# Query and key rows of a hybrid attention block laid out per head in DRAM, with more slots and raw weight buffers

## The chip, the core and the metric

The kernel runs on one core of a Trainium2 chip. The metric is device microseconds of one execution. Engines are named as in the profile: PE is TensorE, DVE VectorE, ACT ScalarE, POOL GpSimd, SP SyncE (here only a DMA queue).

## What is computed

One decoder block over 1024 tokens of width 1024: a root-mean-square norm, one input projection, three attention mixers side by side, an output projection with residual, and a squared-ReLU MLP (width 4096) with residual.

```python
def reference(x, norm_mix, norm_mlp, w_in, ..., w_out, w_up, w_down):
    h = rms_norm(x, norm_mix[l])
    proj = h @ w_in[l]
    a_q, a_kv, a_g, b_qkv, c_qkv = jnp.split(proj, PROJ_SPLITS, axis=-1)
    o_a = nsa_mixer(a_q, a_kv, a_g, ...)        # 4 heads: compressed, selected and window keys
    o_b = dilated_mixer(b_qkv, ...)             # 6 heads in 3 groups of dilation 1, 4, 16
    o_c = stick_breaking_mixer(c_qkv)           # 6 heads, strictly causal
    x = x + jnp.concatenate([o_a, o_b, o_c], axis=-1) @ w_out[l]
    h = rms_norm(x, norm_mlp[l])
    x = x + jnp.square(jax.nn.relu(h @ w_up[l])) @ w_down[l]
```

All heads have 64 dimensions; everything is float32.

## The kernel before

**Precision.** Every matmul operand is split into two parts, hi and lo (a cast on ACT at L103 and a difference on POOL or DVE at L112), and a product is hi·hi + hi·lo + lo·hi. A score needs 64 rows for each part, so hi and lo share the 128 partitions: a key tile is [hi; lo], 64 rows each. `scores` (L633) multiplies it once by the query tile `qh` = [hi; hi] and once by `ql` = [lo; lo], and adds both in PSUM; a masked score has a third small matmul.

**Two streams of work.** A generator `filler` computes the projections, pair of heads by pair of heads, then the output projection and MLP of the first half of the tokens. Between its steps the attention units (`Sb`, `Dil`, `Nsa`; half 0 are tokens 0 to 511, half 1 the rest) are emitted: `spend` hands each unit's cost to the filler. A scheduler then fixes the order on each engine. After the last unit, the second half's output projection and MLP remain: the last 510 us are nearly pure matmul.

**Through DRAM.** The projections' queries, keys and values do not stay in SBUF. `spill_qk` (L540) writes a pair's hi tile and lo tile, 128 rows (two heads) by 512 tokens each, into `q_d` and `k_d`, shaped [pair, hi or lo, 128, 1024]; `spill_v` (L565, L572) writes `v_d`. These stores are issued on the SP queue, between the weight loads. `load_heads` (L605) fetches them for a unit on the POOL queue, into "slots" of 128x1024 from a pool of 11. A query load (L609, L624) reads 64 rows of DRAM twice by an outermost dimension of step 0; a key load (L615, L627) has an outermost dimension of two for hi and lo. A value load (L616, L629) has 128 plain rows. The second-half queries of the NSA heads go through `nq_d` in the same way (L443, L759). `take`, `free` and `live` count slots, and `prefetch` starts the loads of the next units when enough of the 11 are free; the wait for a slot to come free stands on the POOL queue.

**Weights.** `load_w` (L140 on) fetches a group of the input projection in parts of 128x512 into a raw buffer `wraw` (two of them, L168), on the SP queue (L169), and `put` splits a part into `whi` and `wlo` at steps of 4 us of the planner's clock. With two parts in flight, the load of part i+2 is written behind the `put` of part i. In the first 10 us of the planner's clock the order of these loads is fixed as written (`in_order`), among the first weights `w` (L332) and the input `xr` (L349). Later the output projection and MLP weights are loaded at L1045 into `raw`.

Of the kernel before, what the change touches and what calls it, by code (L numbers as in the profile page):

```python
# [16 lines left out]
S, D, HD, DFF = 1024, 1024, 64, 4096  # L17
NB = S // 128
# [41 lines left out]
def tile_trunk(ctx, tc, x, xT, w_in, w_out, w_up, w_down, cw1, cw2, small, t_nsa, t_dil, out):  # L60
# [25 lines left out]
    nq_d = dram.tile([2, 2, 2, 64, 512], F32, name="nq_d")  # L86
    q_r, k_r, v_r, nq_r = [t.bitcast(F32R) for t in (q_d, k_d, v_d, nq_d)]
# [31 lines left out]
    slots = actx.enter_context(tc.tile_pool(name="slots", bufs=11))  # L119
# [12 lines left out]
    def slot(name, dt=F32R):  # L132
        return slots.tile([128, S], dt, tag="slot", name=name)
# [7 lines left out]
    def load_w(key):  # L141
# [69 lines left out]
    DMA, SB0 = 4.0, 8.0  # L211
    FLIP, START, END = 1.3, 5.0, 2.5
    SLOTS = 11
# [215 lines left out]
    def nsa_q(W_q, half):  # L429
# [6 lines left out]
        def fin(p):  # L436
            tp = pair_T(v2, 128 * p)
            if half == 1:
# [3 lines left out]
                for part, t in enumerate((hi, lo)):  # L442
                    nc.sync.dma_start(nq_d[p, part].rearrange("h d t -> (h d) t"), t.bitcast(F32))  # L443
                return
            nsa['q', 0, p] = hi, lo = [slot(n).rearrange("p (h t) -> p h t", h=2) for n in ("nqh", "nql")]
            for i, r in ((0, A), (1, B)):
                put(hi[A, i], lo[A, i], tp[r], qg[r, 2 * p + i:2 * p + i + 1])
                nc.scalar.copy(hi[B, i], hi[A, i].bitcast(F32))
                nc.vector.tensor_copy(lo[B, i], lo[A, i].bitcast(F32))
# [87 lines left out]

    def spill_qk(pair, j, cs, hi, lo):
        for part, t in enumerate((hi, lo)):
            nc.sync.dma_start((q_d, k_d)[j][pair, part, :, cs], t.bitcast(F32))  # L540
# [52 lines left out]
    def rows_of(t, *dims):  # L593

        return bass.AP(tensor=t.tensor, offset=t.offset, ap=[list(d) for d in dims])

    def load_heads(pair, half, heads=(0, 1)):

        q0, nk = 512 * half, 512 * (half + 1)
        ks = slice(0, nk)  # L600
        n = len(heads)
        hs = slice(heads[0], heads[0] + n)
        halves = lambda t: t.rearrange("p (h s) -> p h s", h=2)
        part, twice = (128 * S, 2), (0, 2)
        if n == 1:  # L605
            r = 64 * heads[0]
            qq = halves(slot("qq"))
            for i in range(2):
                nc.gpsimd.dma_start(qq[:, i], rows_of(q_r[pair, i, r:r + 64, q0:q0 + 512], twice, (S, 64), (1, 512)))  # L609
# [3 lines left out]
            else:  # L613
                k, v = slot("k"), slot("v")
            nc.gpsimd.dma_start(k, rows_of(k_r[pair, 0, r:r + 64, ks], part, (S, 64), (1, nk)))  # L615
            nc.gpsimd.dma_start(v, v_r[pair, heads[0], :, ks])  # L616
            return [(qq[:, 0], qq[:, 1], k, v)]
        qh, ql = [halves(slot(nm)) for nm in ("qh", "ql")]
        k, v = [[t[:, 0], t[:, 1]] if half == 0 else [t, slot(nm)]
                for nm in "kv" for t in [halves(slot(nm)) if half == 0 else slot(nm)]]  # L620
# [840 lines left out]
```

## Time and profile before

| | |
|---|---|
| median of 3 runs | 1473.87 us (1472.23 to 1474.32) |
| profiled execution, its own time | 1478.49 us |
| its span | 1476.7 us |
| mean granted clock of TensorE | 0.953 of full speed |
| PE busy | 1347.3 us (91%), 7241 matmuls |
| DVE, POOL, ACT busy | 836.8, 684.3, 647.7 us |
| DMA on the SP queue (hardware) | 136.45 MB in 91808 packets |
| DMA on the POOL queue (software) | 33.85 MB in 86656 packets |
| all packets | 178572, of them 89376 under 512 B |

The profile is of one execution, 4.6 us longer than the median of the runs. It is read by stage here: an opening to 54 us, the projections with the first units to 481 us, the units of half 0 and the NSA heads to 777 us, the last units beside the first half's output projection and MLP to 966 us, and the second half's output projection and MLP. A row of a timeline has the start, the length, the engine and line, the instruction and its tiles, and in brackets the idle time before it with what ended that.

### The profile page before, as it was taken

What the parts mean: (1) busy time and instruction counts of PE and PEld (TensorE: products, weight loads), DVE (VectorE), ACT (ScalarE), POOL (GpSimd) and SP (SyncE); (2) the same over time, 40 slices, a digit from 0 to 9 for tenths busy, and PEclk for the clock granted to TensorE, in tenths of its full rate; (3) what the DMA queues carried; (4) which work ended last, traced back from release to release, by engine and by line L of the source; (5) the groups of instructions that cost most, each with busy time, mean ns of one, the idle gap of its engine ahead of it and who ended that gap; (6) DMA issues with size and microseconds to landing.
All of it is one profiled execution on the core that took longest, in us unless ns stands there. A gap on an engine that the chain in (4) does not pass through costs nothing.

```text
span 1476.7 us, 21132 instructions
## 1 busy us (share of the span) xinstructions
PE 1347.3 (91%) x7241; PEld 1156.5 (78%) x7241; DVE 836.8 (57%) x1973; ACT 647.7 (44%) x1453; POOL 684.3 (46%) x614
## 2 busy tenths in 40 slices
PE   8887978688797999999997696999999999999998
PEld 6876978688786887888886585788888888888887
DVE  7365664468566998888885353783453332332333
ACT  6234554357454666555564142553343222222221
POOL 2123224434673424454556252534755555556553
PEclk9999989899798999999999798999999999999999
DMA  5697566852734422244548545224434333333332
GB/s 180 166 187 192 143 148 152 152 134 61 136 95 144 137 62 61 73 119 115 122 113 146 94 110 110 75 62 136 123 111 145 89 100 94 92 100 92 95 100 86
DMA packets 178572, 171.65 MB, mean 116 GB/s; under 512 B 89376, under 2 KB 105248, under 8 KB 178464
## 3 DMA queue, kind: packets, MB, share of 16 engines
q1 hardware_dynamic: 91808, 136.45, 32.5%
q0 software_dynamic: 86656, 33.85, 13.0%
q8 instruction: 57, 0.93, 0.3%
q14 instruction: 51, 0.42, 0.1%
HBM read 142.67 MB, written 27.30 MB: 115 GB/s over the span
## 4 chain that ended last, share of the span: by engine, by line
PE 67%; DMA 13%; DVE 11%; issue 4%; ACT 4%; SPq 1%; POOL 1%; DVEq 0%; ACTq 0%; POOLq 0%
PE pd L1094 25%; PE pd L1160 23%; DMA wraw<-in_w_in_dram 6%; PE pd L250 6%; PE ptp L684 3%; DMA k<-k_d 2%; PE pd L258 2%; PE po L705 2%; PE po L700 2%; PE pscore L642 1%; PE pscore L639 1%; DMA xch<-stx 1%; DMA wraw<-in_cmp_w_dram 1%; ACT whi L103 1%; DVE b L864 1%
## 5 line engine op out<-in xcount | busy, mean ns | idle before, releaser
L112 POOL TENSOR_TENSOR wlo<-raw,whi 128x512 fp32r<-128x512 f32 x264 | 351.1, 1350 | 370.9 <-ACT whi L103 365.6
L1094 PE MATMUL pd<-whi,hid 128*128 128x512 f32 x1120 | 381.6, 401 | 4.1 <-DVE acc L1099 2.6
L1099 DVE SCALAR_TENSOR_TENSOR acc<-pd,rs,acc 128x512 f32<-128x512 f32 x256 | 191.0, 747 | 117.5 <-PE pd L1094 116.6
L1094 PEld LDWEIGHTS pd<-whi,hid 128*128 128x128 f32 x1120 | 212.2, 189 | 51.9 <-DVE acc L1099 4.3
L103 ACT CAST whi<-raw 128x512 fp32r<-128x512 f32 x264 | 150.6, 619 | 180.7 <-issue 87.8
L1094 PE MATMUL pd<-wlo,hid 128*128 128x512 f32 x560 | 221.7, 396 | 0.0
L1160 PE MATMUL pd<-h_hi,whi 128*128 128x512 f32 x512 | 203.2, 397 | 0.2 <-ACT h_hi L105 0.2
L1160 PE MATMUL pd<-h_lo,whi 128*128 128x512 f32 x512 | 203.0, 398 | 0.0
L1160 PE MATMUL pd<-h_hi,wlo 128*128 128x512 f32 x512 | 202.3, 395 | 0.0
L1164 DVE TENSOR_TENSOR sqr<-sqr 128x512 f32<-128x512 f32 x64 | 49.4, 772 | 263.0 <-ACT sqr L1163 262.7
L250 PE MATMUL pd<-whi,hT_hi 128*128 128x256 f32 (+1 forms) x512 | 155.4, 307 | 15.7 <-DVE vs L114 7.4
L250 PE MATMUL pd<-wlo,hT_hi 128*128 128x256 f32 (+1 forms) x512 | 153.1, 300 | 1.4 <-DVE wlo L112 1.4
L250 PE MATMUL pd<-whi,hT_lo 128*128 128x256 f32 (+1 forms) x512 | 151.7, 298 | 0.0
L1163 ACT ACTIVATE sqr<-pd 128x512 f32<-128x512 f32 x64 | 38.2, 597 | 211.6 <-PE pd L1160 211.6
L1094 PEld LDWEIGHTS pd<-wlo,hid 128*128 128x128 f32 x560 | 106.3, 190 | 20.2
L250 PEld LDWEIGHTS pd<-whi,hT_hi 128*128 128x128 f32 x512 | 104.1, 204 | 17.3 <-DVE vs L114 8.0
L1160 PEld LDWEIGHTS pd<-h_hi,wlo 128*128 128x128 f32 x512 | 97.0, 190 | 22.5
L1160 PEld LDWEIGHTS pd<-h_hi,whi 128*128 128x128 f32 x512 | 97.1, 190 | 22.1 <-ACT h_hi L105 0.7
L1160 PEld LDWEIGHTS pd<-h_lo,whi 128*128 128x128 f32 x512 | 96.4, 189 | 21.3
L112 DVE TENSOR_TENSOR pTlo<-ptp,pThi 128x512 fp32r<-128x512 f32 (+2 forms) x160 | 101.1, 638 | 19.5 <-ACT pThi L103 18.5
L250 PEld LDWEIGHTS pd<-wlo,hT_hi 128*128 128x128 f32 x512 | 105.2, 206 | 1.6 <-DVE wlo L112 1.6
L250 PEld LDWEIGHTS pd<-whi,hT_lo 128*128 128x128 f32 x512 | 104.5, 204 | 0.0
(279 smaller groups left out, 2585.7 us busy)
## 6 DMA issues: line engine op xcount, KB each, us to landing
raw<-in_w_down_dram SPq DMA_DIRECT2D x128, 256.0 KB, 2.9
raw<-in_w_up_dram SPq DMA_DIRECT2D x124, 256.0 KB, 2.9
wraw<-in_w_in_dram SPq DMA_DIRECT2D x66, 256.0 KB, 3.0
k<-k_d POOLq DMA_DIRECT2D x12, 512.0 KB, 19.8
v<-v_d POOLq DMA_DIRECT2D x12, 512.0 KB, 16.1
qh<-q_d POOLq DMA_DIRECT2D x20, 256.0 KB, 11.4
ql<-q_d POOLq DMA_DIRECT2D x20, 256.0 KB, 13.0
v_d<-vs SPq DMA_DIRECT2D x32, 128.0 KB, 3.0
```

The source lines that it names most:

```text
L103: nc.scalar.copy(dst, src)
L112: eng.tensor_tensor(dst_lo, src, dst_hi.bitcast(F32), op=OP.subtract)
L250: nc.tensor.matmul(ps[:, :n], tokens(a, d, tb), b, start=(d == 0 and j == 0), stop=(d == 7 and j == 2))
L258: nc.tensor.matmul(ps, a, b[half][:, d], start=(d == 0 and j == 0), stop=(d == 7 and j == 2))
L684: nc.tensor.transpose(tp[:, off:off + 128], a, ident)
L700: nc.tensor.matmul(po[:, o0:o0 + w], vst, hi[:, src:src + w], start=(e == 0), stop=False)
L705: nc.tensor.matmul(*rest, start=False, stop=last and s not in held)
L1094: nc.tensor.matmul(ps, a[:, cs], b, start=(k == 0), stop=(k == last))
L1099: nc.vector.scalar_tensor_tensor(acc[:, tb, os_], ps, r2[:, t:t + 1], acc[:, tb, os_], op0=OP.mult, op1=OP.add)
L1160: nc.tensor.matmul(ps, a[:, ds], b[:, d], start=(d == 0 and j == 0), stop=(d == 7 and j == 2))
L1163: nc.scalar.activation(h, ps, AF.Relu)
L1164: nc.vector.tensor_tensor(h, h, h, op=OP.mult)
```

## The change

1. The pool of slots has 12 in place of 11, and there are four raw weight buffers in place of two (`RAWS`): `load_w` issues up to four parts at once, and part i+4 stands behind the `put` of part i.
2. `q_d`, `k_d` and `nq_d` hold for each head 128 rows [hi; lo]. `spill_rows` writes a 128-row tile as two stores of 64 rows, one for each head. A group's `spill_qk` issues four stores in place of two: 24 groups give 48 more, and the NSA queries 4 more, 104 in place of 52, all on the SP queue.
3. The query tiles in SBUF are q1 = [hi; lo] and q2 = [lo; hi]; keys stay [hi; lo]. The two matmuls of a score give hi·hi + lo·lo and lo·hi + hi·lo: the same four products, and the same number of matmuls.
4. Loads have plain rows: q1 in one DMA of 128 rows (both heads together), q2 in two of 64 rows, keys and values of half 0 in one DMA for both heads, of half 1 in one for each head. The POOL queue issues 86 loads in place of 104. No load has a leading dimension of 2 or a step of 0.
5. The scratch memory of the software-issued DMA is set to 8192 bytes.

```diff
@@ (slots, raw buffers)
+SLOTS = 12
+RAWS = 4
-    nq_d = dram.tile([2, 2, 2, 64, 512], F32, name="nq_d")
+    nq_d = dram.tile([2, 2, 128, 512], F32, name="nq_d")
-    slots = actx.enter_context(tc.tile_pool(name="slots", bufs=11))
+    slots = actx.enter_context(tc.tile_pool(name="slots", bufs=SLOTS))
@@ load_w
-            raw = wpool.tile([128, 2 * WMAX], F32, tag="wraw", bufs=2, name="wraw")[:, :m]
+            raw = wpool.tile([128, 2 * WMAX], F32, tag="wraw", bufs=RAWS, name="wraw")[:, :m]
-        raws = [load(p) for p in parts[:2]]
+        raws = [load(p) for p in parts[:RAWS]]
-                if i + 2 < len(parts):
-                    raws.append(load(parts[i + 2]))
+                if i + RAWS < len(parts):
+                    raws.append(load(parts[i + RAWS]))
@@ spills
+    def spill_rows(dst, step, t):
+        for h, rows in ((0, A), (1, B)):
+            ap = bass.AP(tensor=dst.tensor, offset=dst.offset + h * step, ap=[list(e) for e in dst.ap])
+            nc.sync.dma_start(ap, t[rows].bitcast(F32))
     def spill_qk(pair, j, cs, hi, lo):
-        for part, t in enumerate((hi, lo)):
-            nc.sync.dma_start((q_d, k_d)[j][pair, part, :, cs], t.bitcast(F32))
+        for rows, t in ((A, hi), (B, lo)):
+            spill_rows((q_d, k_d)[j][pair, 0, rows, cs], 128 * S, t)
@@ load_heads
+    def fetch(t, src):
+        nc.gpsimd.dma_start(t.bitcast(F32), src)
+    def fetch_q(q1, q2, src):
+        fetch(q1, src)
+        fetch(q2[A], src[B])
+        fetch(q2[B], src[A])
-        for i, t in enumerate((qh, ql)):
-            for h in heads:
-                r = 64 * h
-                nc.gpsimd.dma_start(t[:, h], rows_of(q_r[pair, i, r:r + 64, q0:q0 + 512], twice, (S, 64), (1, 512)))
-        for h in heads:
-            r = 64 * h
-            nc.gpsimd.dma_start(k[h], rows_of(k_r[pair, 0, r:r + 64, ks], part, (S, 64), (1, nk)))
-        for h in heads:
-            nc.gpsimd.dma_start(v[h], v_r[pair, h, :, ks])
+        q = [halves(slot(nm)) for nm in ("q1", "q2")]
+        fetch_q(*q, by_head(q_d[pair], qs))
+        for nm, d in (("k", k_d), ("v", v_d)):
+            if half == 0:
+                t = halves(slot(nm))
+                fetch(t, by_head(d[pair], ks))
+            else:
+                t = [slot(nm) for _ in heads]
+                for h in heads:
+                    fetch(t[h], d[pair, h, :, ks])
@@ the program
-    nc = _bacc.Bacc("TRN2", target_bir_lowering=False, num_devices=1)
+    nc = _bacc.Bacc("TRN2", target_bir_lowering=False, num_devices=1, dynamic_dma_scratch_size=8192)
```

Two places show how the order on a queue moves. The first is the SP queue in the opening: `wraw` are parts of the input projection's weights (L169 before, L170 in the change), `w_243` and `w_253` are weights of the first group (L332), and `xr` is the input. Before:

```order
L169 DMA wraw<-in_w_in_dram 128x512 x2
L349 DMA xr<-in_xT_dram 128x1024
L332 DMA w_243<-in_w_in_dram 128x512
L349 DMA xr<-in_xT_dram 128x1024
L332 DMA w_253<-in_w_in_dram 128x512
L169 DMA wraw<-in_w_in_dram 128x512 x2
L349 DMA xr<-in_xT_dram 128x1024 x3
L169 DMA wraw<-in_w_in_dram 128x512 x2
```

In the change:

```order
L170 DMA wraw<-in_w_in_dram 128x512 x4
L349 DMA xr<-in_xT_dram 128x1024
L170 DMA wraw<-in_w_in_dram 128x512
L332 DMA w_243<-in_w_in_dram 128x512
L349 DMA xr<-in_xT_dram 128x1024
L332 DMA w_253<-in_w_in_dram 128x512
L170 DMA wraw<-in_w_in_dram 128x512
L349 DMA xr<-in_xT_dram 128x1024 x3
L170 DMA wraw<-in_w_in_dram 128x512 x2
```

Four raw loads now stand together, and a fifth, which needs the first raw buffer back, stands ahead of `w_243`, the next `xr` and `w_253`.

The second is the POOL queue in the late stage, at the loads for the second dilated unit (`Dil(1, 1)`: queries qh and ql, or q1 and q2, keys and values of a head pair, and `qq` of a single head), between the differences `wlo` and `hid` of the output projection and MLP. Before:

```order
L624 DMA qh<-q_d 128x1x512
L112 TENSOR_TENSOR wlo<-raw,whi 128x512
L624 DMA qh<-q_d 128x1x512
L112 TENSOR_TENSOR wlo<-raw,whi 128x512 x3
L112 TENSOR_TENSOR hid<-sqr,hid 128x512
L112 TENSOR_TENSOR wlo<-raw,whi 128x512 x2
L112 TENSOR_TENSOR hid<-sqr,hid 128x512
L624 DMA ql<-q_d 128x1x512 x2
L627 DMA k<-k_d 128x1x1024 x2
L629 DMA v<-v_d 128x1024
L112 TENSOR_TENSOR wlo<-raw,whi 128x512 x2
L629 DMA v<-v_d 128x1024
```

In the change:

```order
L113 TENSOR_TENSOR wlo<-raw,whi 128x512 x4
L113 TENSOR_TENSOR hid<-sqr,hid 128x512
L113 TENSOR_TENSOR wlo<-raw,whi 128x512 x2
L113 TENSOR_TENSOR hid<-sqr,hid 128x512
L600 DMA k<-k_d 128x1024 x2
L600 DMA v<-v_d 128x1024 x2
L113 TENSOR_TENSOR wlo<-raw,whi 128x512 x2
L600 DMA qq<-q_d 128x512
L600 DMA qq<-q_d 64x512 x2
L600 DMA k<-k_d 128x1024
L600 DMA v<-v_d 128x1024
```

The pair's query loads have moved ahead of this piece, its two key loads and two value loads stand together, and the single head's queries are one load of 128 rows and two of 64. On TensorE, 42 matmuls of L1094 (L1100 in the change) stand between the score that sets free the last stick-breaking pair's first key slot and the first score that reads that slot's new keys; before there were 24.

## Rows read from the trace of the kernel before

**Rows 1.** The page, busy time of TensorE (us, share, instructions) and DMA in 40 slices.
```profile
PE 1347.3 (91%) x7241; PEld 1156.5 (78%) x7241; DVE 836.8 (57%) x1973; ACT 647.7 (44%) x1453; POOL 684.3 (46%) x614
...
DMA  5697566852734422244548545224434333333332
```

**Rows 2.** Windows: start:end, length, busy us of each engine, granted clock, DMA share, GB/s.
```profile
54.00:481.00 427.00, 356.01 (x2416) 332.82 (x2417) 256.46 (x795) 207.55 (x540) 175.80 (x190) 0.89 0.61 144
...
777.00:966.00 189.00, 150.88 (x740) 127.02 (x739) 98.24 (x208) 70.05 (x146) 79.73 (x67) 0.88 0.52 103
966.00:1476.70 510.70, 506.61 (x2245) 412.09 (x2244) 196.90 (x279) 163.57 (x306) 279.44 (x218) 1.00 0.34 103
```

**Rows 3.** Chain of waits that ended last, 54 to 481 us; start, us, what.
```profile
by line: DMA wraw<-in_w_in_dram 21.8%; PE pd L250 21.7%; PE pd L258 5.6%; issue 4.1%; DMA k<-k_d 3.7%; DMA xch<-stx 3.3%; DMA wraw<-in_cmp_w_dram 3.0%; PE ptp L684 2.5%; ACT whi L103 2.5%; DMA v_d<-vs 2.5%; DVE wlo L112 1.9%; SPq L572 1.8%;
...
75.63 15.76 DMA k<-k_d
...
193.82 12.26 DMA wraw<-in_w_in_dram
```

**Rows 4.** The page, DMA issues: count, KB each, median us to landing.
```profile
wraw<-in_w_in_dram SPq DMA_DIRECT2D x66, 256.0 KB, 3.0
k<-k_d POOLq DMA_DIRECT2D x12, 512.0 KB, 19.8
```

**Rows 5.** DMA view, 190 to 207 us, issues and landing.
```profile
wraw<-in_w_in_dram SPq DMA_DIRECT2D x3, 256.0 KB, 9.5
...
k<-k_d POOLq DMA_DIRECT2D x2, 256.0 KB, 12.6
```

**Rows 6.** DMA view, 860 to 863.4 us, 40 slices and one load.
```profile
GB/s 0 0 0 0 0 0 0 0 0 0 337 145 0 48 96 193 193 241 193 482 193 482 193 241 482 289 434 386 386 434 338 243 101 103 32 33 80 53 52 52
...
v<-v_d POOLq DMA_DIRECT2D x1, 512.0 KB, 3.9
```

**Rows 7.** DMA view, 863.6 to 865.8 us, 40 slices.
```profile
GB/s 78 40 40 77 39 40 78 3 77 77 39 38 38 75 37 37 112 112 74 112 74 112 74 149 74 112 112 112 74 112 112 112 74 149 74 112 112 112 74 112
```

**Rows 8.** Timeline of TensorE about 820 us; start, us, instruction, idle before.
```profile
820.48 0.55 PE L639 MATMUL pscore<-k,qh 128*128 128x256 f32 x1 [16.92 <-issue]
...
823.44 0.55 PE L639 MATMUL pscore<-k,qh 128*128 128x256 f32 x1 [2.19 <-issue]
```

**Rows 9.** Timeline of TensorE about 899 us.
```profile
899.22 0.45 PE L639 MATMUL pscore<-k,qh 128*128 128x128 f32 x1 [13.30 <-DMA k<-k_d]
```

**Rows 10.** Timeline of the GpSimd queue, 794 to 829 us; start, us to issue.
```profile
796.38 1.59 POOL L627 DMA_DIRECT2D k<-k_d  x2
```

**Rows 11.** DMA view, 794 to 829 us, landing of the key loads.
```profile
k<-k_d POOLq DMA_DIRECT2D x3, 512.0 KB, 24.0
```

**Rows 12.** Windows, two stretches of the late stage at the lower clock.
```profile
808.24:828.72 20.48, 6.05 (x16) 4.75 (x17) 0.00 (x0) 0.00 (x0) 0.93 (x1) 0.50 1.00 126
...
890.16:903.81 13.65, 4.59 (x14) 3.95 (x15) 0.38 (x1) 0.33 (x1) 0.00 (x0) 0.50 0.61 123
```

**Rows 13.** Waits of TensorE, 54 to 481 us: total us, times, longest.
```profile
PE po L700 <- ACT pThi L103: 19.0, 4, 7.4
...
PE pscore L639 <- DMA k<-k_d: 5.5, 1, 5.5
```

**Rows 14.** Waits of the SyncE queue, whole span.
```profile
SPq L169 <- DVE wlo L112: 69.3, 25, 15.7
```

**Rows 15.** Timeline of the SyncE queue, 3 to 20 us.
```profile
6.38 0.70 SPq L332 DMA_DIRECT2D w<-in_w_in_dram  x1
...
16.24 0.94 SPq L169 DMA_DIRECT2D wraw<-in_w_in_dram  x2
```

**Rows 16.** Timeline of ScalarE, 12 to 26 us.
```profile
16.93 0.60 ACT L103 CAST whi<-w 128x512 fp32r<-128x512 f32 x1
```

**Rows 17.** Line 540, the spills: ns to issue, us to landing.
```profile
L540 SPq DMA_DIRECT2D k_d<-tlo x12: 319/358/667, 58.8 to 478.5; - x12
...
DMA to landing us min/median/max: 2.0/2.8/10.7
```

More of the change, by code (lines that the diff above doesn't have):

```diff
@@ L210, in tile_trunk @@
     pending = []
-    DMA, SB0 = 4.0, 8.0
+    DMA, SPILL = 4.0, 8.0
     FLIP, START, END = 1.3, 5.0, 2.5
-    SLOTS = 11
     live = [2]
@@ L441, in fin @@
                     put(hi[r], lo[r], tp[r], qg[r, 2 * p + i:2 * p + i + 1])
-                for part, t in enumerate((hi, lo)):
-                    nc.sync.dma_start(nq_d[p, part].rearrange("h d t -> (h d) t"), t.bitcast(F32))
+                for rows, t in ((A, hi), (B, lo)):
+                    spill_rows(nq_d[p, 0, rows], 128 * 512, t)
                 return
-            nsa['q', 0, p] = hi, lo = [slot(n).rearrange("p (h t) -> p h t", h=2) for n in ("nqh", "nql")]
+            nsa['q', 0, p] = q1, q2 = [slot(n).rearrange("p (h t) -> p h t", h=2) for n in ("nq1", "nq2")]
             for i, r in ((0, A), (1, B)):
-                put(hi[A, i], lo[A, i], tp[r], qg[r, 2 * p + i:2 * p + i + 1])
-                nc.scalar.copy(hi[B, i], hi[A, i].bitcast(F32))
-                nc.vector.tensor_copy(lo[B, i], lo[A, i].bitcast(F32))
+                put(q1[A, i], q1[B, i], tp[r], qg[r, 2 * p + i:2 * p + i + 1])
+                nc.scalar.copy(q2[B, i], q1[A, i].bitcast(F32))
+                nc.vector.tensor_copy(q2[A, i], q1[B, i].bitcast(F32))
         for p in range(2):
@@ L534, in tile_trunk @@
     t_sel, t_edge, t_cmp, vm = ntab[:, 0:S], ntab[:, S:S + 128], ntab[:, S + 128:S + 192], ntab[:, S + 192:S + 193]
+    def spill_rows(dst, step, t):
+        for h, rows in ((0, A), (1, B)):
+            ap = bass.AP(tensor=dst.tensor, offset=dst.offset + h * step, ap=[list(e) for e in dst.ap])
+            nc.sync.dma_start(ap, t[rows].bitcast(F32))
     def spill_qk(pair, j, cs, hi, lo):
[L539 to L540 removed]
+        for rows, t in ((A, hi), (B, lo)):
+            spill_rows((q_d, k_d)[j][pair, 0, rows, cs], 128 * S, t)
     def end_T(src, pair, j, half):
@@ L590, in spill_dqk @@
             later(6.0, lambda j=j, g=g: fin(j, g))
-    def rows_of(t, *dims):
-        return bass.AP(tensor=t.tensor, offset=t.offset, ap=[list(d) for d in dims])
+    def fetch(t, src):
[4 more added lines that the diff above has]
+        fetch(q2[B], src[A])
     def load_heads(pair, half, heads=(0, 1)):
[L599 to L602, printed above, removed]
+        qs, ks = slice(512 * half, 512 * half + 512), slice(0, 512 * half + 512)
         halves = lambda t: t.rearrange("p (h s) -> p h s", h=2)
-        part, twice = (128 * S, 2), (0, 2)
-        if n == 1:
-            r = 64 * heads[0]
+        by_head = lambda d, cs: d[:, :, cs].rearrange("h p s -> p h s")
+        if len(heads) == 1:
+            h = heads[0]
             qq = halves(slot("qq"))
-            for i in range(2):
-                nc.gpsimd.dma_start(qq[:, i], rows_of(q_r[pair, i, r:r + 64, q0:q0 + 512], twice, (S, 64), (1, 512)))
+            fetch_q(qq[:, 0], qq[:, 1], q_d[pair, h, :, qs])
             if half == 0:
@@ L614, in load_heads, with scores @@
                 k, v = slot("k"), slot("v")
[L615 to L616 removed]
+            fetch(k, k_d[pair, h, :, ks])
+            fetch(v, v_d[pair, h, :, ks])
             return [(qq[:, 0], qq[:, 1], k, v)]
[L618 to L632 removed]
+        q = [halves(slot(nm)) for nm in ("q1", "q2")]
+        fetch_q(*q, by_head(q_d[pair], qs))
+        kv = []
+        for nm, d in (("k", k_d), ("v", v_d)):
+            if half == 0:
+                t = halves(slot(nm))
+                fetch(t, by_head(d[pair], ks))
+                t = [t[:, 0], t[:, 1]]
+            else:
+                t = [slot(nm) for _ in heads]
+                for h in heads:
+                    fetch(t[h], d[pair, h, :, ks])
+            kv.append(t)
+        return [(q[0][:, h], q[1][:, h], kv[0][h], kv[1][h]) for h in heads]
+    def scores(q1, q2, n, k, masked=False):
         ps = ps_s()
@@ L755, in load @@
             if self.slots:
-                qs = nsa['q', 1, self.hp] = [slot(nm).rearrange("p (h t) -> p h t", h=2) for nm in ("nqh", "nql")]
-                for part, t in enumerate(qs):
-                    for i in range(2):
-                        nc.gpsimd.dma_start(t[:, i], rows_of(nq_r[self.hp, part, i], (0, 2), (512, 64), (1, 512)))
+                qs = nsa['q', 1, self.hp] = [slot(nm).rearrange("p (h t) -> p h t", h=2) for nm in ("nq1", "nq2")]
+                fetch_q(*qs, nq_d[self.hp].rearrange("h p t -> p h t"))
         def end(self):
@@ L769, in branch @@
             n, h = self.n, 2 * self.hp + i
-            (qh, ql), sl, st = [t[:, i] for t in nsa['q', self.half, self.hp]], SLOPES[6 + h], self.st[i]
+            (q1, q2), sl, st = [t[:, i] for t in nsa['q', self.half, self.hp]], SLOPES[6 + h], self.st[i]
             prev = None
@@ L849, in weights @@
         def weights(self, n, c0):
-            qh, ql, k, _ = self.head
+            q1, q2, k, _ = self.head
             Wn = 128 * (n + 1)
@@ L1220, in filler @@
         in_order(nc.sync.dma_start(dtab, t_dil))
-        later(SB0, lambda: done.add(('sb', 0)))
+        later(SPILL, lambda: done.add(('sb', 0)))
         W = next_w()
```

21 lines of the change are left out of this document (9 added, 12 removed).

## The prediction

> **What bounds the kernel now.** I read the page first: TensorE is busy for 1347.3 us of 1476.7 [rows 1], so some 129 us at most are idle time, and the high digits of DMA stand mostly in the first third. The windows by stage then say where the idle time lies [rows 2]: 427.0 - 356.0 = 71 us between 54 and 481 us, 189.0 - 150.9 = 38 us between 777 and 966 us, and only 4 us in the last 511 us. In the same two stages the granted clock is 0.89 and 0.88, in the last it is 1.00. A mean of 0.89 between the two levels shown, 1.0 (2.4 GHz) and 0.50 (1.2 GHz), is 22% of the 427 us, 94 us, at the lower level. So I ask what ends the waits of these two stages.
>
> In the middle stage the chain of waits [rows 3] names mostly loads: the raw weights 21.8% and 3.0%, keys 3.7%, the value spills 2.5%, together 31% of 427 us. The chain has 17 pieces of raw weights, which make 24.8% or 105.9 us. A raw weight load lands in 3.0 us as its median over the program [rows 4], but the pieces reach 12.26 us [rows 3]. What stands beside the long ones is the transfer of head loads: from 190 to 207 us three raw loads took 9.5 us, while key loads of the same size took 12.6 us [rows 5].
>
> Why are head loads slow? A 512 KB key load takes 19.8 us [rows 4]. A value load of the same size, on the same queue, with little beside it, took 3.9 us, and the 40 slices under it reach 482 GB/s [rows 6]. Two query loads alone, just behind it, moved 37 to 149 GB/s [rows 7]. The two forms differ in their outermost dimension: 128 rows for the value, a dimension of 2 for queries and keys. So **the form of the load, not its bytes, sets its time**, and it holds others up: in the middle stage the DMA engines are busy to 0.61 and move only 144 GB/s [rows 2].
>
> In the late stage TensorE stood still for 16.92 us, 2.19 us [rows 8] and 13.30 us [rows 9]. The first is put down to "issue", but the key loads were issued from 796.38 us on [rows 10], loads there land in 24.0 us [rows 11], and 796.4 + 24.0 = 820.4 is when the score began. The last is named as a key load. These 32.4 us wait for key loads, and behind them TensorE runs at 0.50 of its clock for 6.05 and 4.59 us of work [rows 12].
>
> **The change part by part.**
>
> *The loads' form (and per-head rows in DRAM).* All 80 query and key loads lose their outermost 2. Their price in the new form is not shown. From below it is the 3.9 us of the value load that stood nearly alone [rows 6], from above the 12.6 us that a 256 KB key load took in company [rows 5]. I take 4 to 6 us, near the value load, since that has the same rows and sizes; several will stand in one queue.
>
> Late stage: in the change 42 matmuls of 512 columns stand between the key slot's release and its next use, at the pace of the last stage (506.6 / 2245 = 0.226 us) [rows 2] 9.5 us; before it was 24, 5.4 us, against a landing of 24.0 us [rows 11]. A load of 4 to 6 us is covered, so the 32.4 us go; one of 12.6 us would leave about 3 us in each of two places. Of the work at half clock, half its time comes back: (6.05 + 4.59) / 2 = 5.3 us. I leave 2 us for what is late next, the value loads behind the keys on the GpSimd queue. Sum 32.4 + 5.3 - 2 = **-36 us**; bounds -24 (the stalls half filled again at the dearer price, and no clock) and -38.
>
> Middle stage: what the chain spends above the quiet landing is 105.9 - 17 x 3.0 = 54.9 us for raw weights. Keys are 3.7%, 15.8 us, one piece [rows 3], 11.8 us above a load of 4 us. Value spills are 2.5%, 10.7 us, 7.7 us above 3.0. Together 74 us. I take two thirds, **-50 us**. The rest goes to what ends next: ScalarE's casts and the transposes that wait for them, which already end 19.0 us of TensorE's waits, whereas a key load ends just 5.5 us of them by name [rows 13], and the small exchange through DRAM (`xch`, 3.3%). Bounds: 5.5 us, if all else is a chain of ScalarE and VectorE; and 71 us of idle time plus the price of the lower clock, at most 94 us x 0.83 busy / 2 = 39 us, so 110 us.
>
> *Four raw buffers.* SyncE waited 69.3 us for a difference to free a raw buffer, 25 times [rows 14]; with four parts in flight this wait moves behind the fourth. It is in the same chain as the raw landings, so I count it in the two thirds and add nothing. It has a price in the opening: a fifth raw load now stands ahead of `w_243`, and needs the first raw buffer, which came free at 16.24 us [rows 15]. So `w_243`, issued at 6.38 us before [rows 15], issues near 17.2 us, lands 3.0 us later [rows 4] at 20.2, and its cast, at 16.93 us before [rows 16], is 3.3 us late; the `xr` behind it too. I take **+4 us**. Bounds 0 (the cast of the first raw part comes earlier) and 10 (16.24 - 6.38, all of it on the path).
>
> *Doubled spills.* 52 more stores on SyncE. One takes 0.36 us to issue [rows 17], so 52 x 0.36 = 19 us of a queue that mostly waits. They stand ahead of weight loads, but with two more raw buffers a load of 3.0 us has slack. I take **+2 us**; bounds 0 and 19.
> The Trainium skill speaks against this part: "DMA: Bandwidth & Descriptors", Rules for kernel authors, calls two transfers to disjoint partition halves not worth it, since they share the same 16 engines and serialize, and asks for one transfer of 128 partitions. By that each pair costs a second transfer's time, not only its issue; the fourth case below is that. No run here shows a half store, so the trace neither agrees nor differs yet.
>
> *Twelfth slot, the queries' rows, fewer loads.* A slot more lets `prefetch` start a little earlier; q1 and q2 take the same matmuls; 18 loads fewer save about 0.8 us of issue each on GpSimd [rows 10], beside `wlo` work that is not late. In the middle stage they are part of the two thirds, in the late stage of the 36; nothing more.
>
> **The sum.** On the profiled execution: 1478.5 - 50 - 36 + 4 + 2 = 1398.5 us. That execution is 4.6 us above the median of the runs, so the median becomes **1394 us**.
>
> **The rivals.**
>
> *A, the forecast* (0.62): 1372 to 1420 us, from 28 us more or 20 us less given back in the middle stage and the shift of the small terms.
>
> *B, only the late stage gains* (0.16). For it: in the middle stage only 5.5 us of TensorE's waits end in a load by name [rows 13], and the casts and transposes would simply queue. Against it: 15.76 and 12.26 us pieces of the chain [rows 3] are plain transfers. Then -50 becomes 0: 1394 + 50 = 1444 us.
>
> *C, the middle stage loses all its transfer excess and most of its clock price* (0.13): 74 + 20 (half of 39) = 94 in place of 50, so 1394 - 44 = 1350 us. For it: the clock of 0.89 falls behind idle time. Against: casts and exchanges remain.
>
> *D, the half stores take the place of the load waits, slower* (0.05). The mechanism is one queue of stores whose halves run one after another: the 52 extra stores each cost a whole landing, at least 2.0 us [rows 17], and the weight loads behind them wait: 52 x 2.0 = 104 us against the 80 us won, 1394 + 104 = about 1498 us. It decides the sign when a pair costs more than 80 / 52 = 1.5 us beyond what it does now. Against it: a store takes 0.36 us to issue [rows 17], the queue goes on without its landing, and the same bytes move.
>
> *E, the change does not do what it says* (0.04). Loads of 64 rows, or with both heads in the middle dimension, might still move at the rate of the queries now [rows 7]. Then nothing is won and about 6 us are lost in the opening and the spills, while two raw buffers win a little: 1474 us.
>
> **How the numbers follow.** 0.2%, about 3 us, is what a measurement of this kernel can tell from no change. A, B and C lie below 1471 us: 0.62 + 0.16 + 0.13 = 0.91, and a hundredth of E: faster 0.92. E gives the rest of no change, 0.03. D is slower, 0.05. The range holds A, the nearer two thirds of B and of C, and the bounds of the small terms: 1346 to 1450 us. The forecast stays the likeliest, 1394 us.
>
> **What would show it.** In the changed profile, key and query loads of 512 KB should land in 4 to 8 us (19.8 before), packets under 512 B should fall by more than half, and the late stage should show no wait of TensorE over 5 us: its 38 us of idle time at most 8, its clock near 1.0. The middle stage should be about 377 us long with a DMA share well below 0.61 and raw loads on the chain near 3 us. The opening should end 3 to 5 us later, with a gap of ScalarE ahead of the cast of the third `w`. The sum is wrong if the middle stage keeps its 427 us although the loads are fast (then B), if SyncE's weight loads stand behind slow half stores (then D), or if key loads still take over 12 us (then E).

## The result and the profile after

The change takes 1377.71 us as the median of 4 runs (1374.45 to 1379.91), against 1473.05 us (1468.67 to 1474.32) of the kernel before on the same chip: a ratio of 0.9356, 95% interval 0.9328 to 0.9384. The medians differ by 95.3 us; the forecast was 1394 us, some 79 us faster.

The page of the profiled execution of the change: busy time, the granted clock in 40 slices, the packets, and the two large DMA queues.

```profile
span 1372.7 us, 21206 instructions
...
PE 1320.4 (96%) x7241; PEld 1128.5 (82%) x7241; DVE 852.1 (62%) x1973; ACT 648.5 (47%) x1453; POOL 660.2 (48%) x596
...
PEclk9999999899999999999999999999999999999999
...
DMA packets 102316, 171.37 MB, mean 125 GB/s; under 512 B 18240, under 2 KB 34112, under 8 KB 102208
...
q1 hardware_dynamic: 92640, 136.45, 34.2%
q0 software_dynamic: 9568, 33.56, 8.1%
```

TensorE is idle for 1372.7 - 1320.4 = 52 us, where it was 129 us [rows 1], and its busy time is 27 us shorter for the same 7241 matmuls, since the clock stays up. The packets of the software queue, which carries the head loads, fell from 86656 to 9568 for about the same bytes, and packets under 512 B from 89376 to 18240. By the packet records of the traces, 73344 of the software queue's packets before had 4 bytes, so hardly any data; in the change these are 1376. The page's DMA issues:

```profile
wraw<-in_w_in_dram SPq DMA_DIRECT2D x66, 256.0 KB, 3.3
k<-k_d POOLq DMA_DIRECT2D x17, 512.0 KB, 5.7
v<-v_d POOLq DMA_DIRECT2D x17, 512.0 KB, 5.0
q<-q_d POOLq DMA_DIRECT2D x10, 512.0 KB, 6.1
```

A 512 KB key load lands in 5.7 us, a query load in 6.1, a value load in 5.0; the key loads took 19.8 us [rows 4]. All loads of the heads together (shortest, median, longest):

```profile
DMA to landing us min/median/max: 3.2/6.0/10.2
```

To compare stages I cut both traces at the same counts of matmuls: the starts of the 233rd, 2649th, 4261st and 5001st, which in the kernel before are the bounds used above to within a us. Two windows of the kernel before at these bounds (columns as in [rows 2]):

```profile
54.60:481.10 426.50, 356.07 (x2416) 332.86 (x2417) 256.06 (x793) 207.19 (x540) 175.80 (x190) 0.89 0.61 144
777.50:966.70 189.20, 151.08 (x741) 127.18 (x740) 98.44 (x209) 70.65 (x147) 79.23 (x67) 0.88 0.52 103
```

The windows of the change:

```profile
0.00:58.40 58.40, 43.51 (x233) 35.91 (x233) 28.73 (x57) 29.40 (x46) 8.92 (x17) 0.95 0.50 158
58.40:408.70 350.30, 332.11 (x2416) 312.22 (x2417) 264.38 (x788) 206.35 (x542) 163.87 (x175) 0.97 0.63 175
408.70:712.40 303.70, 298.86 (x1612) 252.27 (x1611) 260.91 (x634) 176.05 (x410) 134.44 (x124) 0.99 0.32 96
712.40:864.10 151.70, 144.24 (x744) 120.31 (x742) 87.33 (x197) 67.78 (x139) 76.03 (x70) 0.99 0.44 130
864.10:1372.70 508.60, 501.69 (x2243) 407.75 (x2241) 210.78 (x300) 168.91 (x319) 276.96 (x213) 1.00 0.34 102
```

The middle stage went from 426.5 to 350.3 us, its clock from 0.89 to 0.97; the late stage from 189.2 to 151.7 us, its clock from 0.88 to 0.99. In the middle stage TensorE's idle time fell from 426.5 - 356.1 = 70.4 us to 350.3 - 332.1 = 18.2 us, and its busy time by 24.0 us for the same 2416 matmuls. The opening is 3.8 us longer, the stage between is 7 us longer, the last one 1 us shorter. The chain of waits from 54 to 410 us, about the middle stage, answers to [rows 3]:

```profile
by line: PE pd L250 24.0%; issue 4.7%; PE ptp L692 3.8%; PE pd L258 3.4%; DMA xch<-stx 2.7%; PE po L708 2.6%; DMA wraw<-in_w_in_dram 2.5%; DMA q_d<-thi 2.5%; PE po L713 2.4%; DMA k_d<-thi 2.1%; PE pscore L650 2.1%; DVE st L792 1.9%; ACT whi
...
205.38 9.01 DMA wraw<-in_w_in_dram
```

Parts of `w_in` are 2.5% of it, nearly all of that one piece of 9.01 us, and key loads are gone from the front; TensorE's own matmuls lead.

In the late stage no wait of TensorE for a load is left. Its longest waits there (total us, times, longest) are for an activation:

```profile
PE pd L1100 <- ACT sqr L1169: 3.6, 2, 3.0
```

The loads for the second dilated unit, on the GpSimd queue:

```profile
746.26 0.57 POOL L600 DMA_DIRECT2D k<-k_d  x1 [1.99 <-PE pscore L650]
748.76 0.55 POOL L600 DMA_DIRECT2D k<-k_d  x1 [1.93 <-PE pscore L650]
749.30 1.05 POOL L600 DMA_DIRECT2D v<-v_d  x2
```

and the landings there, which answer to the 24.0 us of [rows 11]:

```profile
k<-k_d POOLq DMA_DIRECT2D x3, 512.0 KB, 4.1
v<-v_d POOLq DMA_DIRECT2D x3, 512.0 KB, 6.0
```

The opening shows the fifth raw load ahead of the third first weight, on SyncE:

```profile
16.15 0.33 SPq L170 DMA_DIRECT2D wraw<-in_w_in_dram  x1
16.52 0.43 SPq L332 DMA_DIRECT2D w<-in_w_in_dram  x1
```

and what it does to the cast of that weight on ScalarE, which stood at 16.93 us [rows 16]:

```profile
19.43 0.62 ACT L104 CAST whi<-w 128x512 fp32r<-128x512 f32 x1 [2.23 <-DMA w<-in_w_in_dram]
22.64 1.34 ACT L106 ACTIVATE hT_hi<-xr,sm_t 128x512 fp32r<-128x512 f32 x2 [2.59 <-DMA xr<-in_xT_dram]
```

### The profile page after: what moved, and what is told of

Its sections match the earlier page's. It is cut to its first block, busy times and chain, and to the rows that moved or that the text cites. A ratio compares the mean times of both kernels' runs of the same rounds, so it can differ in the third digit from the quotient of the medians.

```text
span 1372.7 us, 21206 instructions
## 1 busy us (share of the span) xinstructions
PE 1320.4 (96%) x7241; PEld 1128.5 (82%) x7241; DVE 852.1 (62%) x1973; ACT 648.5 (47%) x1453; POOL 660.2 (48%) x596
## 3 DMA queue, kind: packets, MB, share of 16 engines
q0 software_dynamic: 9568, 33.56, 8.1%
## 4 chain that ended last, share of the span: by engine, by line
PE 72%; DVE 11%; DMA 5%; ACT 2%; issue 2%; SPq 1%; DVEq 0%; ACTq 0%
PE pd L1100 28%; PE pd L1166 24%; PE pd L250 6%; PE ptp L692 4%; PE po L713 2%; PE po L708 2%; DMA xch<-stx 2%; PE pscore L650 2%; PE pscore L647 2%; DVE b L870 1%; PE pd L258 1%; DVE pTlo L113 1%; DVE acc L1105 1%; DVE p L663 1%; DMA wraw<-in_w_in_dram 1%
## 5 line engine op out<-in xcount | busy, mean ns | idle before, releaser
L1100 PE MATMUL pd<-whi,hid 128*128 128x512 f32 x1120 | 381.2, 401 | 7.9 <-DVE acc L1105 3.8
L1100 PEld LDWEIGHTS pd<-whi,hid 128*128 128x128 f32 x1120 | 211.0, 189 | 56.8 <-DVE acc L1105 5.9
L1100 PE MATMUL pd<-wlo,hid 128*128 128x512 f32 x560 | 221.0, 395 | 0.0
L1170 DVE TENSOR_TENSOR sqr<-sqr 128x512 f32<-128x512 f32 x64 | 54.1, 845 | 226.4 <-ACT sqr L1169 226.4
L250 PE MATMUL pd<-whi,hT_hi 128*128 128x256 f32 (+1 forms) x512 | 148.1, 291 | 8.6 <-DVE vs L115 5.5
L250 PE MATMUL pd<-wlo,hT_hi 128*128 128x256 f32 (+1 forms) x512 | 146.4, 287 | 1.7 <-DVE wlo L113 1.7
L250 PE MATMUL pd<-whi,hT_lo 128*128 128x256 f32 (+1 forms) x512 | 146.2, 286 | 0.0
L1100 PEld LDWEIGHTS pd<-wlo,hid 128*128 128x128 f32 x560 | 105.6, 189 | 20.2
L104 ACT CAST pThi<-ptp 128x512 fp32r<-128x512 f32 (+2 forms) x160 | 86.9, 551 | 64.9 <-PE ptp L692 62.4
L250 PEld LDWEIGHTS pd<-whi,hT_hi 128*128 128x128 f32 x512 | 97.1, 190 | 9.6 <-DVE vs L115 5.9
L250 PEld LDWEIGHTS pd<-wlo,hT_hi 128*128 128x128 f32 x512 | 97.5, 191 | 2.6 <-DVE wlo L113 2.3
```

What stands on the lines that cost most here:

```text
L104: nc.scalar.copy(dst, src)
L250: nc.tensor.matmul(ps[:, :n], tokens(a, d, tb), b, start=(d == 0 and j == 0), stop=(d == 7 and j == 2))
L1100: nc.tensor.matmul(ps, a[:, cs], b, start=(k == 0), stop=(k == last))
L1170: nc.vector.tensor_tensor(h, h, h, op=OP.mult)
```

## The experiments

Two theories were set against each other. One: the outermost dimension of the loads sets their time, and by it the others'. The other: two more raw buffers and a slot more hid the long landings. Then come the price of half stores, of the fifth raw load, and whether more depth still pays. Each ratio is to runs of the kernel before that were measured beside that kernel (their medians lie between 1472.44 and 1475.91 us), while differences between two kernels of the table are differences of medians that were measured apart. All stage lengths are of the profiled execution, in us, between the same counts of matmuls; for raws_only that execution is 8.4 us faster than the median. The order of the work moves with each edit, so a few us between neighbouring stages mean little.

| kernel | median us | ratio to before, interval | opening | middle | next | late |
|---|---|---|---|---|---|---|
| before | 1473.05 | | 54.6 | 426.5 | 296.4 | 189.2 |
| the change | 1377.71 | 0.9356 (0.9328 to 0.9384) | 58.4 | 350.3 | 303.7 | 151.7 |
| layout_only | 1394.36 | 0.946 (0.941 to 0.9511) | 53.7 | 374.9 | 295.6 | 156.7 |
| raws2 (layout and slot) | 1388.59 | 0.942 (0.9381 to 0.946) | 54.0 | 368.3 | 304.1 | 150.9 |
| slots11 (layout and raw buffers) | 1384.75 | 0.9396 (0.9359 to 0.9434) | 58.0 | 356.2 | 299.3 | 159.3 |
| raws_only | 1444.76 | 0.9794 (0.9749 to 0.9839) | 57.3 | 387.8 | 298.2 | 180.6 |
| buffers_only (raw buffers and slot) | 1438.65 | 0.9761 (0.9713 to 0.9809) | 56.7 | 393.6 | 303.1 | 172.0 |
| keys2 | 1411.59 | 0.9575 (0.9528 to 0.9622) | 57.5 | 368.0 | 303.9 | 172.9 |
| store1 | 1537.3 | 1.0437 (1.0393 to 1.048) | 59.5 | 514.7 | 303.3 | 153.6 |
| halves | 1461.05 | 0.992 (0.9894 to 0.9947) | 52.9 | 413.8 | 298.0 | 184.5 |
| opening | 1378.54 | 0.9355 (0.9321 to 0.9388) | 60.8 | 350.6 | 305.3 | 152.0 |
| opening2 | 1371.18 | 0.9299 (0.9262 to 0.9336) | 51.1 | 352.5 | 306.8 | 152.6 |
| slots13 | 1373.93 | 0.9322 (0.9294 to 0.935) | 56.6 | 348.6 | 306.7 | 151.9 |
| raws6 | 1362.25 | 0.9242 (0.9216 to 0.9268) | 56.7 | 338.4 | 302.2 | 149.8 |

### The layout and the loads alone

```diff
-SLOTS = 12
-RAWS = 4
+SLOTS = 11
+RAWS = 2
```

> The change with two raw weight buffers and eleven slots, so the rows of queries and keys and the form of their loads alone. Theory (the form of the loads is what gained): 1380 to 1400 us, key loads landing in 4 to 8 us, no wait of TensorE over 5 us after 770 us. Rival (two more raw buffers and the slot are what hid the long landings): 1430 to 1450 us, with only the late stage's 36 us won.

Measured 1394.36 us, 81.5 us below the kernel before that ran beside it (1475.91 us) and within the theory's range. The late stage fell by 32.5 us and the middle stage by 51.6 us. The window of its middle stage shows 374.9 - 344.0 = 30.9 us of idle time:

```profile
53.70:428.60 374.90, 344.02 (x2416) 322.41 (x2417) 256.61 (x797) 204.32 (x538) 158.56 (x171) 0.94 0.59 163
```

The waits of ScalarE for raw weights did not all go with the long landings (total us, times, longest; first the kernel before, then this one):

```profile
ACT whi L103 <- DMA wraw<-in_w_in_dram: 83.9, 31, 8.9
...
ACT whi L104 <- DMA wraw<-in_w_in_dram: 50.3, 25, 5.9
```

On the chain of waits a raw part still has pieces like this one, where its load lands in 2.9 us in the median:

```profile
212.67 7.91 DMA wraw<-in_w_in_dram
```

So the new rows and the loads' form carry most of the gain, and with two raw buffers ScalarE still waits for a raw part 25 times, 2.0 us each: a part is only asked for when a buffer comes free.

### Buffers and slot alone, and the raw buffers alone

```diff
-slots = actx.enter_context(tc.tile_pool(name="slots", bufs=11))
+slots = actx.enter_context(tc.tile_pool(name="slots", bufs=12))
-    SLOTS = 11
+    SLOTS = 12
-raw = wpool.tile([128, 2 * WMAX], F32, tag="wraw", bufs=2, name="wraw")
+raw = wpool.tile([128, 2 * WMAX], F32, tag="wraw", bufs=4, name="wraw")
-raws = [load(p) for p in parts[:2]]
+raws = [load(p) for p in parts[:4]]
```

The diff is cut: the kernel before gets the smaller scratch memory too, and a second place that takes a raw buffer its number of buffers.

> The kernel before with four raw weight buffers, twelve slots and the smaller scratch memory; rows and loads as before. Theory (form of the loads): 1455 to 1478 us, the late waits of 13 to 17 us for key loads still there, TensorE idle for over 50 us between 54 and 481 us. Rival (depth of buffering): 1410 to 1440 us, with the idle time of the middle stage halved.

Measured 1438.65 us, 37 us faster: the theory's range was missed, and the rival's met in time, though the middle stage's idle time fell only from 70.4 to 47 us. The second kernel leaves the slots at eleven.

> The kernel before with four raw weight buffers and the smaller scratch memory, eleven slots, rows and loads as before. Theory (of the 37 us that buffers and slot won together, the raw buffers won the middle stage's 25 and the slot the late stage's 12): 1446 to 1455 us, the two late waits for keys still at 28 to 33 us, the casts' waits for raw weights under 15 us. Rival (raw buffers won it all): 1435 to 1442 us with the late waits at 20 us.

Measured 1444.76 us, 30 us faster than the kernel before that ran beside it (1474.95 us): the raw buffers won most of it. With them ScalarE's waits for raw weights are nearly gone although head loads are as slow as before:

```profile
ACT whi L103 <- DMA wraw<-in_w_in_dram: 9.9, 6, 3.0
```

But TensorE's wait for keys in the late stage stays with eleven slots,

```profile
785.01 0.55 PE L639 MATMUL pscore<-k,qh 128*128 128x256 f32 x1 [15.53 <-issue]
```

and with the twelfth slot it is shorter (the first of the two waits in buffers_only):

```profile
807.78 0.55 PE L639 MATMUL pscore<-k,qh 128*128 128x256 f32 x1 [9.89 <-issue]
```

The late stage shows the slot: 180.6 us with eleven, 172.0 with twelve. Neither theory was whole: depth hides long landings for 30 to 37 us, the loads' form removes them for 81 us, and the two overlap (37 + 81.5 is 118, together they win 95).

### The change without its raw buffers, and without its slot

```diff
-RAWS = 4
+RAWS = 2
```

> The change with two raw weight buffers in place of four. Theory: 1374 to 1390 us, since a raw load of about 3 us needs no deeper queue and the opening gets its 3.8 us back. Rival: 1400 us or more, with the waits of ScalarE's casts for raw weights back at tens of us.

```diff
-SLOTS = 12
+SLOTS = 11
```

> The change with eleven slots in place of twelve. Theory: 1374 to 1384 us, no difference that can be told, as no wait of TensorE for a load is left. Rival (the slot lets loads start early enough): 1390 us or more, with waits of TensorE for keys in the late stage.

Measured 1388.59 and 1384.75 us: on fast loads the two raw buffers still win 11 us and the slot 7 us, by the medians. The intervals of both ratios overlap with that of the change, by little for raws2, so neither size is firm. The raw buffers' 11 us is at the upper end of the theory's range for raws2, but the rival's sign came: the casts' waits for raw weights are back.

```profile
ACT whi L104 <- DMA wraw<-in_w_in_dram: 56.0, 30, 6.8
```

In the change this wait is 5.2 us, once. The slot's 7 us lies between the two guesses. The rival's sign, waits of TensorE for keys in the late stage, did not come; what the slot saves there is not settled. In the middle stage, from layout_only to slots11, the raw buffers take 374.9 to 356.2 us, and cost the opening 4.3 us.

### Keys alone with the old form

A key's hi and lo blocks stand 65 rows apart, so that a load keeps an outermost dimension of two. The keys of half 0, one load for two heads in the change, become one load for each head, five loads more; their stores stay half stores. The diff is cut to the new rows and the load.

```diff
+    k_d = dram.tile([6, 2, 2, 65, S], F32, name="k_d2")
+    def fetch_k(t, pair, h, ks):
+        b = k_d[pair, h, 0, 0:64, ks]
+        nk = ks.stop - ks.start
+        fetch(t, bass.AP(tensor=b.tensor, offset=b.offset, ap=[[65 * S, 2], [S, 64], [1, nk]]))
```

> The change with key loads alone back in the form with an outermost dimension of two: a key's hi rows and lo rows stand 65 rows apart in DRAM, so that the two blocks stay two; stores, queries, values, buffers and slots as in the change. Theory (the outermost two sets the load's time): key loads land in 10 to 20 us, TensorE waits for keys in the late stage again for 10 to 30 us, 1395 to 1430 us. Rival (it is the rows being stored by head, or the fewer loads, that gained): key loads land in 5 to 7 us, 1374 to 1384 us.

Measured 1411.59 us, 34 us slower than the change, with the late stage at 172.9 us in place of 151.7. The page's issues (KB each, median us to landing):

```profile
v<-v_d POOLq DMA_DIRECT2D x17, 512.0 KB, 11.7
k<-k_d POOLq DMA_DIRECT2D x12, 512.0 KB, 18.0
```

And in the timeline of TensorE in the late stage, the wait for the last stick-breaking keys, 13.30 us before the change [rows 9]:

```profile
857.68 0.44 PE L663 MATMUL pscore<-k,q 128*128 128x128 f32 x1 [8.39 <-DMA k<-k_d]
```

Key loads of the same bytes, from rows that lie alike but for the gap, land in 18.0 us in place of 5.7, and the value loads, whose form did not change, in 11.7 in place of 5.0. The DMA view from 760 to 800 us shows a raw weight caught in it:

```profile
v<-v_d POOLq DMA_DIRECT2D x3, 512.0 KB, 19.8
...
raw<-in_w_down_dram SPq DMA_DIRECT2D x3, 256.0 KB, 10.8
```

The theory holds: the outermost two sets the time of the load, and transfers beside it pay as well. The packet records of the two traces show how. On the GpSimd queue both kernels move the same 8192 packets of 4096 bytes, but in keys2 some are in flight during 260 us, for 50% of it at most four at a time; in the change during 156 us, for 15% of it at most four and for 57% twelve or more. So the data goes in the same pieces, with fewer of them at a time. Of the layout's 81.5 us, keys2 gives 34 back; queries alone in the old form were not tried, and that the rest is theirs is argued, not shown.

### One store with an outermost two, and half stores alone

```diff
-        for h, rows in ((0, A), (1, B)):
-            ap = bass.AP(tensor=dst.tensor, offset=dst.offset + h * step, ap=[list(e) for e in dst.ap])
-            nc.sync.dma_start(ap, t[rows].bitcast(F32))
+        ap = bass.AP(tensor=dst.tensor, offset=dst.offset, ap=[[step, 2]] + [list(e) for e in dst.ap])
+        nc.sync.dma_start(ap, t.bitcast(F32))
```

> The change with each pair of half stores of 64 rows written as one store of 128 rows, whose DRAM side has an outermost dimension of two. Theory (the outermost two slows a store as it slows a load, and 52 issues saved are worth little): stores land in 6 to 12 us in place of 2 to 3, and units that wait for them start later, 1380 to 1400 us. Rival (two half transfers serialize, one is better): 1365 to 1374 us.

Measured 1537.3 us, 160 us slower than the change, far beyond what either expected; all of it is in the middle stage, 514.7 us with a clock of 0.82. The mechanism expected was late stores; what the SyncE queue shows is a queue that stands (start, length of the issues):

```profile
170.95 15.15 SPq L170 DMA_DIRECT2D wraw<-in_w_in_dram  x5
...
188.05 7.17 SPq L570 DMA_DIRECT2D v_d<-vs  x1
```

and in the group of the stores' line, shortest, median and longest issue in ns:

```profile
L541 SPq DMA_DIRECT2D k_d<-tlo x12: 491/4730/7164, 65.5 to 574.8; - x12
```

Five raw weight loads behind such stores take 15.15 us to be issued, 3 us each, and the stores themselves are held for up to 7 us. In the change four raw loads behind half stores take 3.79 us, about 1 us each:

```profile
177.31 3.79 SPq L170 DMA_DIRECT2D wraw<-in_w_in_dram  x4
```

By the packet records of store1, exactly two data packets of this queue are in flight during 9.4 of these 15.15 us. Over the whole middle stage it is one or two for 54% of the time in which the queue moves data, and for 13% in the change: the slow form again moves few packets at a time. GpSimd's head loads then wait for the stores, in its list of waits (total us, times, longest):

```profile
POOL q L599 <- DMA q_d<-tlo: 71.8, 4, 28.4
POOL k L599 <- DMA k_d<-tlo: 48.7, 3, 20.4
```

So, for rows laid out by head, two half stores are not a price here but the cure. What they cost by themselves was tried on the kernel before, whose stores have 128 plain rows:

```diff
-            nc.sync.dma_start((q_d, k_d)[j][pair, part, :, cs], t.bitcast(F32))
+            for r in (A, B):
+                nc.sync.dma_start((q_d, k_d)[j][pair, part, r, cs], t[r].bitcast(F32))
```

The diff is cut: the stores of the NSA queries are halved in the same way.

> The kernel before with each query and key store of 128 plain rows written as two stores of 64 rows to the same place: 52 more stores, nothing else. Theory (a half store costs its issue on a queue that mostly waits): 1473 to 1485 us. Rival (two transfers to disjoint partition halves serialize, each extra one costs a landing of 2 us or more): over 1520 us.

Measured 1461.05 us: 0.992 of the kernel before, so faster by 11 us, which no theory expected. The rows of the stores answer to [rows 17]:

```profile
L542 SPq DMA_DIRECT2D k_d<-tlo x24: 445/590/1342, 57.7 to 466.7; - x24
...
DMA to landing us min/median/max: 2.2/2.7/9.1
```

A half store takes 0.59 us to issue, more than the 0.36 of a whole one, and lands no later. The serialized price is excluded. Why it is faster is open: the scheduler moved other work around the added stores, and no run holds that order still.

### The opening

```diff
-            if clock[0] < 10.0:
+            if clock[0] < 21.0:
                 in_order(i)
```

> The change with the raw loads of the second weight group kept behind the input's loads in the opening (the fixed order holds up to 21 us of the planner's clock in place of 10). Theory (the fifth raw load costs the opening 3.8 us, on the path): 1371 to 1376 us, no idle time of 3 us on TensorE near 20 us. Rival (the delay is made up later): 1376 to 1381 us.

Measured 1378.54 us, no difference. In the change TensorE waits near 20 us and ahead of the first value projection:

```profile
23.41 0.50 PE L258 MATMUL pd<-hT_hi,whi 128*128 128x512 f32 x1 [3.08 <-ACT hT_hi L106]
...
58.35 0.58 PE L250 MATMUL pd<-whi,hT_hi 128*128 128x256 f32 x1 [5.49 <-DVE vs L115]
```

In this kernel the first wait is down to 0.37 us, but the raw loads of the second group now come late, and the second wait is longer:

```profile
55.66 0.58 PE L250 MATMUL pd<-whi,hT_hi 128*128 128x256 f32 x1 [9.73 <-DVE vs L115]
```

In ScalarE's waits up to 60 us (total us, times, longest) the cause stands first:

```profile
ACT whi L104 <- DMA wraw<-in_w_in_dram: 13.1, 1, 13.1
```

Of the 2.7 us won at the first wait nothing is left at the end. A second edit fetches that group earlier as well:

```diff
-        if d == 2:
+        if d in (2, 5):
             fetch_w(2.6)
```

> The change with the second weight group fetched two input rows earlier and its raw loads kept behind the third pair of first weights, so that they stand neither ahead of those nor behind the whole opening. Theory (what was won in the opening was lost again as later raw weights came later): 1372 to 1376 us, with neither 3 us idle near 20 us nor 9 us near 50 us. Rival (this time is covered by what follows): 1376 to 1381 us.

Measured 1371.18 us: 6.5 us below the change by the medians, but its runs spread from 1360.74 to 1376.83 us and the intervals of the two ratios overlap. So that it wins is not clear of the noise. Both idle times shrank (2.90 us ahead of the value projection, 1.04 us near 20), and the opening ends 7 us sooner.

### More depth

```diff
-RAWS = 4
+RAWS = 6
-dynamic_dma_scratch_size=8192
+dynamic_dma_scratch_size=4096
```

> The change with six raw weight buffers (scratch memory 4096 to make room). Theory (with four, ScalarE's casts wait under 10 us for raw weights, so more buffers have nothing to win): 1373 to 1383 us. Rival (depth still pays): under 1370 us.

Measured 1362.25 us, 15 us below the change, and its interval (0.9216 to 0.9268) lies clear of it: **faster than both kernels**, and the theory is wrong. Its middle stage:

```profile
56.70:395.00 338.30, 327.67 (x2416) 307.95 (x2417) 268.05 (x788) 206.85 (x543) 166.51 (x178) 0.98 0.65 183
```

TensorE's idle time there is 338.3 - 327.7 = 10.6 us (18.2 in the change). ScalarE waited only 5.2 us for w_in parts in the change, so this gain was not to be seen in that row; which wait went is not settled. Nor does SyncE's wait for a buffer tell what depth is worth: it does not shrink with more buffers (total us, times, longest; first the change with four, then this kernel with six; it was 69.3 with two [rows 14]).

```profile
SPq L170 <- DVE wlo L113: 55.9, 24, 18.2
...
SPq L170 <- DVE wlo L113: 68.0, 26, 17.8
```

```diff
-SLOTS = 12
+SLOTS = 13
-dynamic_dma_scratch_size=8192
+dynamic_dma_scratch_size=4096
```

> The change with thirteen slots (scratch memory 4096 to make room). Theory (no wait of TensorE for a load is left, so a slot more has little to win): 1372 to 1380 us. Rival (each slot gives some 6 us): 1366 to 1372 us.

Measured 1373.93 us, in the theory's range, 4 us below the change, and the intervals overlap. As this kernel has the same small scratch memory, that alone does not make the 15 us of raws6. Six raw buffers together with the earlier fetch of the second group were not tried.

## Why the prediction was right, point by point

**The direction and the two stages.** The cause was read rightly: the outermost dimension of two made the loads slow, and they held others up. keys2 puts it back for keys alone and gets the slow landings and the late waits back. What was mis-sized is the middle stage, and the raw buffers in it.

**Late stage, -36 us.** Measured -37.5 us, 30.6 of it idle time and 6.8 busy time (forecast 32.4 - 2 and 5.3). The loads land in 4.1 us where I took 4 to 6 [rows 6], and the cover of 42 matmuls was enough. The layout alone gives -32.5; the slot takes most of the rest.

**Middle stage, -50 us.** Measured -76.2 us. The idle time fell by 52.2 us, near the two thirds of the chain's transfer excess. The other 24.0 us are busy time, with the granted clock at 0.97 in place of 0.89. The sum gave half of the work at half clock back in the late stage, but nothing of it here, where it stood only in a bound (39 us) and in rival C (20 us): the sum left this term out without a reason, and it is the larger miss. The layout alone measured -51.6 us (426.5 to 374.9), but as 39.5 us of idle and 12.1 us of busy time, so that it meets the -50 is in part luck. Of the rivals, B (nothing in the middle stage) is excluded by it. C (0.13, 1350 us) overstated what the loads alone could give, but the whole change came part of the way to it, by other means.

**Four raw buffers, "I count it in the two thirds and add nothing".** This step failed too, and it is the same miss seen from the levers: in the middle stage buffers and slot took 24.6 us more than the layout alone, 12.7 of idle and 11.9 of busy time. The waits for raw weights were priced as long landings only. With landings near 3 us ScalarE still waited 50.3 us for them, because a part was asked for only when one of two buffers came free; four buffers took 18.7 us off the middle stage on fast loads (slots11 against layout_only). By the medians they are worth 11 us in the change, after the opening's price. The row to price it by is ScalarE's wait for raw weights: 83.9 us before, 50.3 with the layout alone, 5.2 in the change. SyncE's 69.3 us behind a buffer [rows 14], which I read, do not show it, since that wait is still 55.9 us with four buffers and 68.0 with six.

**The slot, "nothing more".** Worth 7 us, 5.9 in the middle stage and 7.6 in the late one, of which part is given back between.

**The opening, +4 us.** Measured +3.8 us, by the very chain forecast: `w` issued at 16.52 us, its cast at 19.43 in place of 16.93. But it was not a price of the end: the run that removed that wait won nothing, and the run in which the raw loads behind it come sooner too is 6.5 us faster by the medians, not clear of the noise.

**Doubled spills, +2 us, and rival D.** The issue was under-priced: 0.55 us and more for a half store, so by these medians 104 of them take about 57 us against 52 x 0.36 = 19, 38 us more of SyncE's time, not 19. It stayed hidden, and halves shows no loss. The rule that speaks against it, in the Trainium skill's "DMA: Bandwidth & Descriptors", Rules for kernel authors (two transfers to disjoint halves serialize; use one of 128 partitions), does not bear out as a cost here: the median landing is 2.7 us for halves and 2.8 for whole stores. The same table asks for an outermost dimension whose size is a multiple of 16, since a smaller one confines a transfer to at most as many of the engines; 18.0 against 5.7 us for one load, and the two packets in flight in store1, agree with that; where the rules conflict, as in store1, the second one weighs far more (1537.3 against 1377.7 us).

**Signs that did not come.** The middle stage's DMA share was to fall well below 0.61. It is 0.63, because the stage is shorter: 0.61 x 426.5 = 260 us of the engines' time before, 0.63 x 350.3 = 221 us now. The share alone does not tell slow transfers from a short stage. And the one long raw piece left on the chain is 9.01 us, not near 3.

**The sum.** -80 us forecast on the profiled execution, -104 measured there; by the medians -79 and -95. In the terms of the sum, the missing 24 us are the middle stage, which fell 26 us further, by its busy time above all; the other terms, with 7 us more in the stage between, nearly cancel. By the levers, the missing 16 us of the medians are about the raw buffers and the slot: 1394.4 us, the layout without them, is what the forecast named for the whole, and that the two meet so closely is chance.

## What to carry to other kernels

In this kernel a software-issued load with an outermost dimension of two took three times as long as the same bytes in plain rows (18.0 against 5.7 us), and such a store held up the queue that issued it; the price is paid by whatever is in flight beside it or queued behind it; store the data so that loads have 128 rows, even at the price of more and smaller stores. When a chain shows long waits for a transfer, ask both how long it lands and when it was asked for: a faster landing and a deeper buffer are two gains, and the wait of the engine that uses the data prices both, where the queue's own wait for a free buffer does not. When idle time goes, look at the granted clock of the stage as well: here it gave back another 24 us. A wait that is seen at the opening is worth removing only if what moves behind it is not what ends the next wait.

## What was not expected of the hardware

- A hardware-issued store with an outermost two holds up the queue that issues it: five loads behind such stores took 15.15 us to issue and some stores 7 us, whereas such loads on the GpSimd queue before took 0.8 us each to issue [rows 10] and only landed late.
- A store of 64 rows takes longer to issue than one of 128 rows of the same length: 0.59 us against 0.36 us in the median of `k_d<-tlo`, [rows 17] and halves.
- Six raw buffers win 15 us more where ScalarE's waits for raw weights were already down to 5.2 us.
